# The FFN gate's modulation vector is computed during gate and up, by ScalarE and GpSimd

## The chip, the cores and the metric

The kernel runs on one core of one Trainium2 chip. The metric is the device time of one execution in microseconds. Engines are named as the profile names them: PE is TensorE (PEld its weight loads), DVE is VectorE, ACT is ScalarE, POOL is GpSimd, SP is SyncE, which issues most of the DMAs.

## The reference

One layer of a hybrid backbone over 640 tokens (512 latent, 128 context), model width 2048, FFN width 5632, all in fp32:

```
mod = silu(c) @ w_mod + b_mod            # w_mod is 2048 x 12288: six vectors of 2048
sh1, sc1, g1, sh2, sc2, g2 = split(mod, 6)
h = rmsnorm(x) * (1 + sc1) + sh1
p = h @ w_in                              # then RWKV-7 mixing and gMLP
x = x + g1 * (mix @ w_out)
h = rmsnorm(x) * (1 + sc2) + sh2
ff = (silu(h @ w_ffn_gate) * (h @ w_ffn_up)) @ w_ffn_down
y = rmsnorm(x + g2 * ff)
```

mod is made twice, from c for the latent tokens and from c_ctx for the context tokens (v = 0 and 1 in the code). The vector of this case is the last one, g2, number 5: it is used in the last part of the down projection alone.

## The kernel before

**Stages.** (1) Norm of x and the modulation vectors 0 and 1, to 125 us. (2) The input projection, 125 to about 1060 us: 43 column blocks of w_in, four pieces each (`pieces`), multiplied by `win`; between the matmuls run the mixers of RWKV and gMLP, which a small planner in the kernel (`Mixer`, with costs per job and due times counted in matmul steps) interleaves. The modulation vectors 2, 4, 3 and 5 are made here too. (3) The recurrence, (4) the output projection, (5) gate and up, from about 1490 to 2590 us, (6) the down projection, (7) the final norm.

**fp32 by halves.** Wherever a weight is multiplied, it is cut into a high part (`hi`, a ScalarE cast to fp32r, L1465 in gate, up and down) and a low part (`lo`, VectorE: raw minus hi, L1466); the product is hi*x_hi + hi*x_lo + lo*x_hi (L1685, L1686, L1688). hi and lo have three buffers each.

**Modulation vectors in stage 2** (`mod_all`, L939; `load_mod`, L932). For each vector and each pair of 128-row blocks of w_mod, two DMAs of 1 MB bring 2 x 128 x 2048; 8 products with the two columns of silu(c) (`cT`) as weights add up in one PSUM bank (L948). Then the bias comes in, VectorE adds (L965), TensorE turns the rows into columns (L182) and VectorE copies them to `modc[g]`. `mod_all` is a generator; after each piece of w_in it is advanced by MODR = 1.36 steps on average, so that its 204 steps spread over the 160 pieces.

**Gate and up.** `seven` (L1659 on) computes the product of a pair of column blocks with seven instead of eight half products (Strassen's scheme in Winograd's form). One loop turn f handles one block of columns (f = 2 to 43; blocks 0 and 1 are done plainly): per turn 8 weight tiles of 128 x 512 are loaded (`load_w`, L1778; 13 buffers); GpSimd makes 8 combinations of them (`combined`, L1594: `t` and `raw` are outputs), 7 half products o = 0 to 6 follow with 2 parts each, 12 matmuls of 320 columns per part. The results in PSUM are joined in `Gate` (L1830 on), four products late (LAG): VectorE additions with a PSUM operand (L1847, L1851, L1855, L1857, L1861), two of SBUF alone (L1856, L1858), a silu on ScalarE (L1862), a VectorE product (L1863). After every second turn GpSimd makes four combinations of the results (`stores`, L1803 to L1810), and `part` cuts three of them into halves (L1823, L1824). The `yield` of `seven` stands after each half product, so the loop body there can slip in loads.

**Order.** Each engine and the queue of each issuer run in order. Outside the regions with a schedule by hand, the framework's planner sets that order: it places each instruction when its own model of times has the inputs ready, the earlier one in the program first, and adds the semaphores.

**What uses the vector.** `Last` and `End` (L1944, L1997) read `modc[5]` in the last chunk of the down projection.

Of the kernel before, what the change touches and what calls it, by code (L numbers as in the profile page):

```python
# [10 lines left out]
F32 = mybir.dt.float32  # L11
F32R = mybir.dt.float32r
BF16 = mybir.dt.bfloat16
AF = mybir.ActivationFunctionType
ALU = mybir.AluOpType
# [4 lines left out]
P = 128  # L20
D = 2048
KB = D // P
# [24 lines left out]
WAIT = 20  # L47
NW = 8
SUBST = 4.6
MODR = 1.36  # L50
NREC = 8
CHK = (3, 3, 4, 4, 4, 4)
POOLK = (3,)
# [36 lines left out]
def flow_step(ctx: ExitStack, tc, x_prompt, x_sample, state_rwkv, c, c_ctx, w_mod, b_mod,  # L90
# [3 lines left out]
    nc = tc.nc  # L94
    V, S, G, TE = nc.vector, nc.scalar, nc.gpsimd, nc.tensor
# [13 lines left out]
    def tpool(**a):  # L109
        if a.get("space") != DRAM:  # L110
            a["reuse_waits"] = "tile"
        return tc.tile_pool(**a)

    cp = ctx.enter_context(tpool(name="const", bufs=1))
    dp = ctx.enter_context(tpool(name="dram", bufs=1, space=DRAM))
    cbx = ExitStack()
    cb = cbx.enter_context(tpool(name="constb", bufs=1))
# [5 lines left out]
    for h in range(2):  # L123
# [8 lines left out]
                         op0=ALU.mult, op1=ALU.add)  # L132
# [6 lines left out]
    mhalf = cp.tile([P, 1], F32, name="mhalf")  # L139
# [7 lines left out]
    mix = cb.tile([P, 640], F32, name="mix")  # L147
    gs2 = mix[96:128, 0:T]
    modc = {g: cp.tile([P, KB, 2], F32, name=f"modc{g}") for g in (2, 3, 4, 5)}
    cT = cb.tile([P, 2 * KB + 32], F32, name="cT")  # L150

    d_o = dp.tile([KB, P, T], F32, name="d_o")
    d_x1 = dp.tile([KB, P, T], F32, name="d_x1")
# [25 lines left out]
    def mod_cols(pspool, ms, out, tag="pt"):  # L179
        pt = pspool.tile([P, 4, P], F32, tag=tag, name="ptm")  # L180
        for cb in range(4):
            TE.transpose(pt[:, cb, :], ms[:, cb * P:(cb + 1) * P], ident)  # L182
        src = pt.rearrange("p cb (j r) -> p j cb r", r=32)
        for v in range(2):
            V.tensor_copy(out.rearrange("p (j cb) v -> p j cb v", cb=4)[:, :, :, v],
                          src[:, :, :, v])
# [745 lines left out]
    def load_mod(g, kb):  # L932
        quad = cur["pool"].tile([P, 2, 4, 512], F32, tag=cur["raw"], name="wt", bufs=1)
        for u in range(2):
            nc.sync.dma_start(quad[:, u].rearrange("p j n -> p (j n)"),
                              w_mod[0, (kb + u) * P:(kb + u + 1) * P, g * D:(g + 1) * D])
        return quad

    def mod_all():  # L939
        for g in (2, 4, 3, 5):  # L940
            pm = cur["psum"].tile([P, 512], F32, tag="pmod", name=f"pm{g}")
            quad = load_mod(g, 0)
            for _ in range(4):
                yield
            for kb in range(0, KB, 2):
                for u in range(2):
                    for j in range(4):
                        TE.matmul(pm[32 * j:32 * j + 2, :], cT[:, 2 * (kb + u):2 * (kb + u) + 2], quad[:, u, j, :],  # L948
                                  start=(kb + u == 0), stop=(kb + u == KB - 1), tile_position=(0, 32 * j))
                for _ in range(2):  # L950
                    yield
                if kb + 2 < KB:
                    quad = load_mod(g, kb + 2)
                    for _ in range(4):
                        yield
            ms = cur["pool"].tile([P, 2, 4, 512], F32, tag=cur["raw"], name=f"ms{g}", bufs=1)[:, 0, 0, :]
            G.memset(ms, 0.0)
            for j in range(4):
                for v in range(2):
                    nc.sync.dma_start(ms[32 * j + v:32 * j + v + 1, :],  # L960
                                      b_mod[:, g * D + 512 * j:g * D + 512 * j + 512])
            yield
            yield
            for j in range(4):
                V.tensor_add(ms[32 * j:32 * j + 2, :], pm[32 * j:32 * j + 2, :], ms[32 * j:32 * j + 2, :])  # L965
            mod_cols(cur["tp"], ms, modc[g], tag=cur["tag"])
            yield
# [6 lines left out]
    g = 0  # L974
# [21 lines left out]
    def take(b, halves):  # L996

        mixA.finish(b - RAW)
        pr = bp.tile([P, T], F32, tag="praw", name="praw", bufs=RAW)
        for hf in range(2):  # L1000
            S.copy(pr[:, HALF * hf:HALF * hf + HALF], halves[hf])
        mixA.add(blocks[b][1](pr), blocks[b][2], wide[0] + 32 * RAW)
# [18 lines left out]
    for n, (b, q) in list(enumerate(pieces))[N0:]:  # L1021
# [4 lines left out]
        if q == 3:  # L1026
            take(b, halves)
        due += MODR
        while due >= 1.0:
# [442 lines left out]
    with ExitStack() as ph:  # L1472
# [6 lines left out]
                        in1=prm[:, C_N2:C_N2 + KB].unsqueeze(2).to_broadcast([P, KB, 2]), op=ALU.mult)  # L1479
# [51 lines left out]
        for hf in range(2):  # L1531
            s = slice(HALF * hf, HALF * hf + HALF)
            for m in range(KB):
                if hf or m >= AHEAD:
                    four_blocks(hf, m, 0)
                ps = four_blocks(hf, m, 1)
# [8 lines left out]
                if hf and m > 1:  # L1545
                    for kb in HALVES[m - 2:m - 1] if m < 14 else HALVES[2 * m - 16:2 * m - 14]:
                        first_half(kb)
                    if 4 <= m < 12:
                        j, i = divmod(m - 4, 2)
# [34 lines left out]
    pP = ctx.enter_context(tpool(name="pP", bufs=8, space=PSUM))  # L1584
# [121 lines left out]
    def load_down(s):  # L1706
        if s < len(steps):
            c, n = steps[s]
            for b, r, m in (("11", 0, 0), ("21", 1, 0), ("22", 1, 1), ("12", 0, 1)):
                raw = xap.tile([P, 4, P], F32, tag=next(wtags), name="rawd")  # L1710
                r0 = (starts[c] + r * NFF // 2) * P
                nc.sync.dma_start(raw[:, 0:CHK[c], :], w_ffn_down[
                    0, r0:r0 + CHK[c] * P, (2 * n + m) * P:(2 * n + m + 1) * P].rearrange("(k p) n -> p k n", p=P))
                WD[s, b] = raw
                yield
# [55 lines left out]
    def load_w(n):  # L1771
        if n < NFF:
            f = ORDER[n]
            for b, w, k0 in (("11", w_ffn_gate, 0), ("21", w_ffn_gate, 8), ("22", w_ffn_up, 8), ("12", w_ffn_up, 0)):
                for q in range(2):
                    raw = gu.tile([P, 4, P], F32, tag="raw", name="raw", bufs=RAWB)
                    r0 = (k0 + 4 * q) * P
                    nc.sync.dma_start(raw, w[0, r0:r0 + 512, f * P:f * P + P].rearrange("(k p) n -> p k n", p=P))  # L1778
                    WB[n, b, q] = raw
                    yield  # L1780
# [6 lines left out]
    gux = ExitStack()  # L1787
# [42 lines left out]
    class Gate:  # L1830
# [5 lines left out]
        def __call__(self, o, p):  # L1836
# [22 lines left out]
            elif o == 6:  # L1859
# [7 lines left out]
                if f % 2:  # L1867
                    stores(f // 2)

    dloads = itertools.chain(load_down(0), load_down(1))  # L1870
    first_blocks()
    for f in range(2, NFF):
        b = {n: [WB.pop((f, n, q)) for q in range(2)] for n in ("11", "12", "21", "22")}
        bs = b["11"], b["12"], b["21"], b["22"]
        for o in seven(*bs, lambda i, k: X[i, k], Gate(f)):
            if o == 2:
                loads = itertools.chain(loads, load_w(f + 2))
            if o > 2:
                next(loads, None)
                next(loads, None)  # L1880
            if f == NFF - 2 and o == 6:
                load(0, 1)
                load(0, 2)
            if f == NFF - 1:
                now(FIRST_OPS, o)
                if o > 3:
                    next(dloads)
    for _ in range(2):
        next(dloads)
    while hooks:  # L1890
        hooks.pop(0)()
    part(3)
# [238 lines left out]
    for t in (3, 4, 0, 1, 2):  # L2131
        for h in (1, 0):
            out = fin.tile([P, 4, 256], F32, tag=f"out{h}", name="out")
# [3 lines left out]
            else:  # L2137
                V.scalar_tensor_tensor(out=out, in0=src, scalar=rse[:, t:t + 1],
                                       in1=fg[:, 4 * h:4 * h + 4], op0=ALU.mult, op1=ALU.mult)
# [31 lines left out]
```

## Time and profile before

| | us |
|---|---|
| median of 3 runs | 3196.04 |
| lowest and highest | 3189.53, 3201.81 |
| profiled execution, own time | 3191.31 |
| its span, first to last instruction | 3189.5 |

| engine | busy us | share of the span |
|---|---|---|
| PE | 3075.3 | 96% |
| DVE | 2347.6 | 74% |
| ACT | 1474.9 | 46% |
| POOL | 1220.2 | 38% |

The mean granted TensorE clock is 0.991. A row of a group reads: line, engine, operation, output<-inputs, shapes, count | busy us, mean ns of one | idle time of the engine just before these instructions, and what ended it. A row of the timeline reads: start, duration, engine, line, operation, tiles, count [idle time before <- what ended it]. Where instructions of one engine follow each other closely, their spans can overlap a little; start to start is then what one costs. A row of a stretch reads: from:to, length, then for each engine busy us and instructions, then granted clock, DMA share and GB/s.

### The profile page before, as it was taken

What the parts mean: (1) busy time and instruction counts of PE and PEld (TensorE: products, weight loads), DVE (VectorE), ACT (ScalarE), POOL (GpSimd) and SP (SyncE); (2) the same over time, 40 slices, a digit from 0 to 9 for tenths busy, and PEclk for the clock granted to TensorE, in tenths of its full rate; (3) what the DMA queues carried; (4) which work ended last, traced back from release to release, by engine and by line L of the source; (5) the groups of instructions that cost most, each with busy time, mean ns of one, the idle gap of its engine ahead of it and who ended that gap; (6) DMA issues with size and microseconds to landing.
All of it is one profiled execution on the core that took longest, in us unless ns stands there. A gap on an engine that the chain in (4) does not pass through costs nothing.

```text
span 3189.5 us, 72242 instructions
## 1 busy us (share of the span) xinstructions
PE 3075.3 (96%) x28216; PEld 2861.3 (90%) x28216; DVE 2347.6 (74%) x4120; ACT 1474.9 (46%) x3216; POOL 1220.2 (38%) x1065
## 2 busy tenths in 40 slices
PE   6899999999999999999999999999999999999997
PEld 4688878788878888899999999999999999999997
DVE  4566777667775678767877878777777788877788
ACT  3344544454444444346544444444444445444365
POOL 2001121221122024411465666656655655555542
PEclk9999999999999999999999999999999999999999
DMA  9767786777777688475344434443344365553453
GB/s 370 245 192 202 217 231 172 212 199 212 221 202 193 214 275 268 153 210 162 97 125 128 122 107 127 119 121 119 109 130 126 108 194 156 163 160 119 143 165 123
DMA packets 740439, 550.89 MB, mean 173 GB/s; under 512 B 141056, under 2 KB 673504, under 8 KB 731264
## 3 DMA queue, kind: packets, MB, share of 16 engines
q1 hardware_dynamic: 727136, 532.47, 55.3%
q0 software_dynamic: 10624, 13.23, 1.8%
q8 instruction: 222, 3.64, 0.5%
q14 instruction: 121, 0.99, 0.1%
q10 hardware_dynamic: 2336, 0.57, 0.1%
HBM read 437.79 MB, written 110.95 MB: 172 GB/s over the span
## 4 chain that ended last, share of the span: by engine, by line
PE 73%; DVE 10%; issue 6%; DMA 6%; ACT 3%; POOL 2%; SPq 0%; DVEq 0%; POOLq 0%; ACTq 0%
PE P L1688 15%; PE P L1685 15%; PE P L1686 15%; PE big L196 5%; PE big L200 4%; PE big L197 4%; DMA raw<-in_w_in_dram 1%; PE pm L948 1%; DVE lo L1466 1%; PE big L1081 1%; PE big L1524 1%; PE big L1525 1%; PE big L1526 1%; PE big L1082 1%; PE big L1083 1%
## 5 line engine op out<-in xcount | busy, mean ns | idle before, releaser
L1685 PE MATMUL P<-xo,hi 128*128 128x320 f32 x2352 | 700.5, 310 | 0.2 <-ACT hi L1465 0.2
L1686 PE MATMUL P<-xo,hi 128*128 128x320 f32 x2352 | 700.4, 309 | 0.0
L1466 DVE TENSOR_TENSOR lo<-raw,hi 128x512 fp32r<-128x512 f32 x526 | 517.8, 989 | 161.6 <-ACT hi L1465 158.7
L1465 ACT CAST hi<-raw 128x512 fp32r<-128x512 f32 x526 | 326.7, 622 | 468.4 <-PE P L1686 397.6
L1688 PE MATMUL P<-xo,lo 128*128 128x320 f32 x2352 | 441.8, 310 | 4.1 <-DVE lo L1466 4.1
L196 PE MATMUL big<-h_hi,hi 128*128 128x320 f32 x1376 | 438.2, 325 | 7.8 <-ACT hi L174 4.4
L1685 PEld LDWEIGHTS P<-xo,hi 128*128 128x128 f32 x2352 | 442.3, 188 | 0.5 <-ACT hi L1465 0.5
L1686 PEld LDWEIGHTS P<-xo,hi 128*128 128x128 f32 x2352 | 442.7, 188 | 0.0
L197 PE MATMUL big<-h_lo,hi 128*128 128x320 f32 x1376 | 422.6, 314 | 0.8 <-DVE h_lo L360 0.8
L1594 POOL TENSOR_TENSOR raw<-raw 128x512 f32<-128x512 f32 x252 | 410.5, 1638 | 10.1 <-DVE lo L1466 1.8
L1688 PEld LDWEIGHTS P<-xo,lo 128*128 128x128 f32 x2352 | 370.0, 188 | 4.9 <-DVE lo L1466 4.9
L1685 PE MATMUL P<-xd,hi 128*128 128x320 f32 x1232 | 367.8, 310 | 6.1 <-ACT P L2079 2.8
L1686 PE MATMUL P<-xd,hi 128*128 128x320 f32 x1232 | 366.8, 309 | 0.0
L200 PE MATMUL big<-h_hi,lo 128*128 128x320 f32 x1376 | 319.8, 312 | 3.9 <-DVE lo L175 2.1
L196 PEld LDWEIGHTS big<-h_hi,hi 128*128 128x128 f32 x1376 | 261.8, 190 | 58.2 <-issue 26.1
L175 DVE TENSOR_TENSOR lo<-raw,hi 128x512 fp32r<-128x512 f32 x268 | 185.4, 695 | 157.6 <-ACT hi L174 153.9
L1594 POOL TENSOR_TENSOR t<-raw 128x512 f32<-128x512 f32 x84 | 123.7, 1472 | 427.5 <-DMA raw<-in_w_ffn_up_dram 415.9
L1465 ACT CAST hi<-rawd 128x512 fp32r<-128x512 f32 (+1 forms) x288 | 167.1, 586 | 225.3 <-PE P L1686 148.9
L174 ACT CAST hi<-raw 128x512 fp32r<-128x512 f32 x268 | 164.4, 617 | 225.9 <-PE big L197 84.9
L197 PEld LDWEIGHTS big<-h_lo,hi 128*128 128x128 f32 x1376 | 261.6, 190 | 5.8 <-DVE h_lo L360 1.9
L1466 DVE TENSOR_TENSOR lo<-rawd,hi 128x512 fp32r<-128x512 f32 (+1 forms) x288 | 231.9, 812 | 24.9 <-ACT hi L1465 24.2
L1688 PE MATMUL P<-xd,lo 128*128 128x320 f32 x1232 | 236.6, 310 | 4.2 <-DVE lo L1466 4.2
(408 smaller groups left out, 6129.7 us busy)
## 6 DMA issues: line engine op xcount, KB each, us to landing
wt<-in_w_mod_dram SPq DMA_DIRECT2D x96, 1024.0 KB
raw<-in_w_ffn_gate_dram SPq DMA_DIRECT2D x182, 256.0 KB
raw<-in_w_ffn_up_dram SPq DMA_DIRECT2D x182, 256.0 KB
rec<-d_S SPq DMA_DIRECT2D x80, 576.0 KB
raw<-in_w_in_dram SPq DMA_DIRECT2D x172, 256.0 KB
rawd<-in_w_ffn_down_dram SPq DMA_DIRECT2D x128, 256.0 KB
raw<-in_w_out_dram SPq DMA_DIRECT2D x96, 256.0 KB
xd<-d_os SPq DMA_DIRECT2D x66, 320.0 KB
```

Of the source, the lines that this page charges most:

```text
L174: S.copy(hi, raw)
L175: V.tensor_sub(lo, raw, hi.bitcast(F32))
L196: TE.matmul(halves[hf], hi[:, k, :], h_hi[:, kb, s], start=(kb == 0), stop=False)
L197: TE.matmul(halves[hf], hi[:, k, :], h_lo[:, kb, s], start=False, stop=False)
L200: TE.matmul(halves[hf], lo[:, j - 4 * q, :], h_hi[:, j, s], start=False, stop=(j == KB - 1))
L948: TE.matmul(pm[32 * j:32 * j + 2, :], cT[:, 2 * (kb + u):2 * (kb + u) + 2], quad[:, u, j, :], start=(kb + u == 0), stop=(kb + u == KB - 1) ...
L1465: S.copy(hi[:, 0:nk], raw[:, 0:nk])
L1466: V.tensor_sub(lo[:, 0:nk], raw[:, 0:nk], hi[:, 0:nk].bitcast(F32))
L1594: G.tensor_tensor(out=o[:, 0:nk], in0=p[:, 0:nk], in1=q[:, 0:nk], op=ALU.subtract)
L1685: TE.matmul(ps, hi[:, k, :], xk[:, 0, :], start=q == 0 and k == 0 and not filled, stop=False)
L1686: TE.matmul(ps, hi[:, k, :], xk[:, 1, :], start=False, stop=False)
L1688: TE.matmul(ps, lo[:, k, :], x(i, 4 * q + k)[:, 0, :], start=False, stop=q == nq - 1 and k == nk - 1 and last)
```

## The change

Vector 5 leaves `mod_all`; MODR falls from 1.36 to 1.02, which is 1.36 x 3/4. `cT` moves from a pool that closes before gate and up to one that stays. A new generator `gate_mod` makes the vector in gate and up, a quarter (512 channels) at a time. For each of the 16 blocks of 128 rows it loads a 128 x 512 tile of w_mod (256 KB, three buffers, two steps ahead); for each v ScalarE multiplies the tile by the column of silu(c) (one value per partition) and GpSimd adds it to an accumulator `am` (128 x 512, fp32, with the bias in its first row). v = 0 writes a tile of its own (`wc`, one buffer), v = 1 writes over the loaded tile. After 16 blocks, 8 products of 128 x 128 pieces of the accumulators with a column of -0.5 sum over the partitions, in a PSUM bank of the pool that the half products use, and VectorE multiplies by -2 into `modc[5]`. The generator has 36 steps per quarter, and the loop advances it at o = 0, 2, 4, 6; what is left after the last turn is run there.

```
-MODR = 1.36
+MODR = 1.02
...
-    cT = cb.tile([P, 2 * KB + 32], F32, name="cT")
+    cT = cp.tile([P, 2 * KB + 32], F32, name="cT")
...
-        for g in (2, 4, 3, 5):
+        for g in (2, 4, 3):
...
+    gm = gux.enter_context(tpool(name="gm", bufs=1))
+    def gate_mod():
+        ws = []
+        def fetch():
+            i = len(ws)
+            if i < 4 * KB:
+                j, kb = divmod(i, KB)
+                w = gm.tile([P, 512], F32, tag="wm", name="wm", bufs=3)
+                nc.sync.dma_start(w, w_mod[0, kb * P:kb * P + P, 5 * D + 512 * j:5 * D + 512 * j + 512])
+                ws.append(w)
+        fetch()
+        fetch()
+        for j in range(4):
+            ac = [gm.tile([P, 512], F32, tag=f"am{v}", name="am") for v in range(2)]
+            for a in ac:
+                G.memset(a, 0.0)
+                nc.sync.dma_start(a[0:1, :], b_mod[:, 5 * D + 512 * j:5 * D + 512 * j + 512])
+            for _ in range(3):
+                yield
+            for kb in range(KB):
+                fetch()
+                w = ws[KB * j + kb]
+                for v in range(2):
+                    wc = w if v else gm.tile([P, 512], F32, tag="wc", name="wc")
+                    S.activation(wc, w, AF.Copy, scale=cT[:, 2 * kb + v:2 * kb + v + 1])
+                    G.tensor_tensor(out=ac[v], in0=ac[v], in1=wc, op=ALU.add)
+                    yield
+            yield
+            ps = pP.tile([P, 512], F32, tag="P", name="pgm")
+            for k in range(4):
+                for v in range(2):
+                    TE.matmul(ps[:, 2 * k + v:2 * k + v + 1], ac[v][:, P * k:P * k + P], mhalf, start=True, stop=True)
+            V.tensor_scalar(modc[5][:, 4 * j:4 * j + 4, :].rearrange("p k v -> p (k v)"), ps[:, 0:8], -2.0, None,
+                            op0=ALU.mult)
+    gmod = gate_mod()
...
+            if o % 2 == 0:
+                next(gmod, None)
...
+    for _ in gmod:
+        pass
```

## The prediction

> **What bounds the kernel now.** First the busy time by stretch, for the two stages that the change touches: the input projection (125 to 1030 us), which loses work, and gate and up (1560 to 2480 us), which gets it.
>
> ```profile
> core 0: us, PE busy (x) PEld busy (x) DVE busy (x) ACT busy (x) POOL busy (x), PEclk, DMA share, GB/s
> 125.00:1030.00 905.00, 873.99 (x10139) 750.95 (x10139) 627.69 (x1257) 440.81 (x936) 155.39 (x255) 0.99 0.73 204
> 1560.00:2480.00 920.00, 920.00 (x6264) 920.00 (x6263) 707.21 (x879) 396.63 (x690) 567.60 (x374) 1.00 0.40 119
> ```
>
> TensorE sets the pace of both: 97% busy in the first, without a gap in the second, at granted clock 1.00. One column block f of gate and up is 7 products x 2 parts x 12 = 168 matmuls, so 6264 matmuls are 37.3 blocks and one block takes 920/37.3 = 24.67 us. VectorE (77%), ScalarE (43%) and GpSimd (62%) look as if they had room there. Whether GpSimd's room is real is the question of this case, so next come the groups of that stretch.
>
> ```profile
> L1466 DVE TENSOR_TENSOR lo<-raw,hi 128x512 fp32r<-128x512 f32 x448 | 450.6, 1010 | 140.1 <-ACT hi L1465 137.5 <-issue 0.4
> L1594 POOL TENSOR_TENSOR raw<-raw 128x512 f32<-128x512 f32 x226 | 368.6, 1641 | 7.2
> L1594 POOL TENSOR_TENSOR t<-raw 128x512 f32<-128x512 f32 x75 | 109.5, 1459 | 346.2 <-DMA raw<-in_w_ffn_up_dram 334.8 <-DVE lo L1466 7.6 <-DVE act L1824 2.1
> L1465 ACT CAST hi<-raw 128x512 fp32r<-128x512 f32 x446 | 277.2, 622 | 414.3 <-PE P L1686 358.8 <-issue 17.7 <-POOL raw L1594 15.5
> L1824 DVE TENSOR_TENSOR act<-act,sp 128x320 fp32r<-128x320 f32 x57 | 47.3, 829 | 0.0
> L1857 DVE TENSOR_TENSOR pq<-P,pq 128x320 f32<-128x320 f32 x37 | 18.2, 491 | 1.3
> L1803 POOL TENSOR_TENSOR s<-act 128x320 f32<-128x320 f32 x19 | 24.8, 1308 | 0.0
> ```
>
> VectorE's subtraction for the low part (L1466, two operands in SBUF) has a mean of 1010 ns. The timeline of VectorE shows what it takes undisturbed: it starts, and 0.60 us later the next instruction does.
>
> ```profile
> 1823.36 0.48 DVE L1824 TENSOR_TENSOR act<-act,sp 128x320 fp32r<-128x320 f32 x1
> 1823.76 0.48 DVE L1851 TENSOR_TENSOR act<-P,act 128x320 f32<-128x320 f32 x1
> 1824.16 0.68 DVE L1466 TENSOR_TENSOR lo<-raw,hi 128x512 fp32r<-128x512 f32 x1
> 1824.76 0.48 DVE L1824 TENSOR_TENSOR act<-act,sp 128x320 fp32r<-128x320 f32 x1
> ...
> 1829.57 0.83 DVE L1863 TENSOR_TENSOR act<-act,c 128x640 f32<-128x640 f32 x1 [0.21 <-ACT c L1862]
> 1830.31 0.69 DVE L1466 TENSOR_TENSOR lo<-raw,hi 128x512 fp32r<-128x512 f32 x1
> 1831.90 1.22 DVE L1466 TENSOR_TENSOR lo<-raw,hi 128x512 fp32r<-128x512 f32 x1 [0.91 <-ACT hi L1465]
> ```
>
> In the quiet part of these rows GpSimd rests, by the first of its own rows for 8.38 us up to 1831.26:
>
> ```profile
> 1831.26 1.30 POOL L1594 TENSOR_TENSOR t<-raw 128x512 f32<-128x512 f32 x1 [8.38 <-DMA raw<-in_w_ffn_up_dram]
> 1832.52 1.33 POOL L1803 TENSOR_TENSOR s<-act 128x320 f32<-128x320 f32 x1
> ```
>
> Where it works back to back, the same instruction comes every 8.61/5 = 1.72 us (1.71 without the tail of the last), and GpSimd's own subtraction every 6.87/4 = 1.72:
>
> ```profile
> 1937.51 8.61 DVE L1466 TENSOR_TENSOR lo<-raw,hi 128x512 fp32r<-128x512 f32 x5
> ```
>
> ```profile
> 1935.29 6.87 POOL L1594 TENSOR_TENSOR raw<-raw 128x512 f32<-128x512 f32 x4
> ```
>
> So the two take turns on something, 0.60 us the one and 1.71 - 0.60 = 1.11 us the other, and do not overlap. Instructions that read PSUM are not held up: L1857 keeps a mean of 491 ns against 0.48 undisturbed, while L1824, with both operands in SBUF, has 829 against 0.48.
>
> The Trainium skill, page "SBUF — State Buffer", section "Who interferes with whom", states this as a rule: a VectorE instruction with two SBUF inputs and a GpSimd instruction that reads SBUF need one shared port, held by one of them for the whole instruction. The rows agree (1.71 is the sum, not the larger of the two). It speaks against putting additions on GpSimd here: by it the change costs at least the +23 us worked out below, by a port that both could read through at once it would cost nothing there.
>
> **The change, part by part.**
>
> *Taken from the input projection.* For g = 5: eight pairs of 1 MB loads, 8 x 16 matmul instructions (L948), four transposes (L182), small bias loads, four VectorE additions on two partitions. TensorE's timeline shows one such group and the transposes of one vector:
>
> ```profile
> 749.11 0.30 PE L533 MATMUL pmm<-lsum,bones 128*128 128x320 f32 x1
> 749.34 1.90 PE L948 MATMUL pm<-wt,cT 128*2 128x512 f32 x16
> 751.17 0.42 PE L196 MATMUL big<-h_hi,hi 128*128 128x320 f32 x1
> 751.43 0.31 PE L197 MATMUL big<-h_lo,hi 128*128 128x320 f32 x1
> ```
>
> ```profile
> 793.09 0.60 PE L182 MATMUL ptm<-ident,ms 128*128 128x128 f32 x4
> ```
>
> From L533 to L197 is 2.32 us; the two matmuls that start in it besides the group need 0.146 each (24.67/168), so the group costs 2.03 us. Eight make 16.2 us, with the transposes 16.8. MODR 1.02 spreads three vectors over the same blocks, so nothing gets denser. TensorE is 97% busy in this stage, so I take all of it: **-16.8 us**. Bounds: 0 if other waits fill it, -24 if the idle time ahead of L948 goes too, (71.8 + 25.0)/4:
>
> ```profile
> L948 PE MATMUL pm<-wt,cT 128*2 128x512 f32 x512 | 71.8, 592 | 0.0
> L948 PEld LDWEIGHTS pm<-wt,cT 128*2 128x2 f32 x512 | 10.3, 83 | 25.0 <-issue 24.1 <-PE big L197 0.2
> ```
>
> *Added to gate and up.* The generator advances at o = 0, 2, 4, 6, four steps per block; 36 steps make a quarter, so 144 steps fill 36 blocks, f = 2 to 37. Most steps are one ScalarE multiply (128x512) and one GpSimd addition (128x512). In the 36 blocks:
>
> ScalarE, at L1465's 622 ns, gets 4 x 0.62 = 2.5 us per block; 43% busy becomes 53%, and it waits for TensorE before most casts anyway (358.8 us of its idle time). Cost 0 while that cover holds.
>
> GpSimd gets four additions with two SBUF operands, like L1594. I count the shared resource per block of 24.67 us. GpSimd has 8 wide subtractions ((226 + 75)/37.3) and 2 narrow ones (four per two blocks). VectorE has 14 L1466, 1.5 L1824, L1856, L1858 and L1863. A wide pair is 1.71. A narrow GpSimd instruction holds 0.73: L1803 ends at 1832.52 + 1.33 = 1833.85, and VectorE's 1831.90 instruction before it ended at 1833.12.
>
> Before: 8 x 1.71 + 2 x (0.73 + 0.60) + 4 further L1466 x 0.60 + 3.5 x 0.40 + 0.74 = 13.7 + 2.7 + 2.4 + 2.1 = 20.9 us of 24.67. After: the four L1466 that stood alone become pairs, 12 x 1.71 + 2.7 + 2.1 = 25.3 us. That is more than the 24.67 that TensorE needs: the port becomes the bound, by 0.6 us per block at the least. VectorE has five additions per block that read PSUM (L1847, L1851, L1855, L1857, L1861), 5 x 0.40 (L1851 above) = 2.0 us; they leave the port free, and only those that fall into a GpSimd turn are hidden. GpSimd's turns are then 10.3 + 4.4 = 14.7 us, some 57% of a block, so 43% of 2.0 = 0.9 us is exposed: 26.2 us. Ends: 25.3 (all hidden) and 27.3 (none). Per block +1.5 us, times 36: **+55 us**; ends +23 and +95. The low parts have three buffers, so VectorE can fall behind by about two parts (3.5 us) before TensorE stands, which is gone within three blocks. TensorE's gaps should then stand ahead of L1688, released by L1466.
>
> On the rate of one addition the Trainium skill's page "GPSIMD Engine Reference", section 4.1, says GpSimd is about twice as slow as VectorE for two inputs; an estimate from that is 1.20 us per turn, 25.7 us per block at the least and 14 us more in all. The row's 1.11 is used.
>
> SyncE gets 64 loads of 256 KB and 8 of 2 KB. With three buffers, a load waits for the last addition of the tile three before; behind it stand the weight loads (L1778), which mostly wait for VectorE themselves, and for those GpSimd waits (334.8 us at t, above). 16.8 MB over 36 blocks add 18 GB/s to 119. I cost this at 0; if GpSimd's turn comes later for it, that is part of the upper end.
>
> ```profile
> SPq L1778 <- DVE lo L1466: 355.5, 186, 10.8
> ```
>
> Four times, TensorE runs 8 products with one column, whose weights are the accumulators. Each is two matmul instructions (L948: 512 for 256 calls); at L182's 0.15 us, 64 make 9.6 us. While TensorE waits for VectorE anyway they cost nothing; in a stage that it bounds, up to 9.6 us. They also wait for the last addition, one step earlier in the program, and hold one of eight PSUM banks: 0 to one GpSimd turn of 1.7 us each, 0 to 7 us; taken as 0. The move of cT issues nothing. The 8 memsets on GpSimd are some 0.5 us each, over 900 us: 0.
>
> *Sum.* 3191.3 (the profiled execution's own time) - 16.8 + 55 = 3229.5 us. The median of the runs shown, 3196.0, lies 4.7 above that execution; on its scale the forecast is **3234 us**.
>
> **The rivals.**
>
> *The port has room after all* (not slower). The sequence 1.71 was seen for five turns at most; if GpSimd slips its additions into VectorE's idle time (140 us ahead of L1466 in 920), blocks stay at 24.67. For it: VectorE is 77% busy. Against: free port time is 24.67 - 20.9 = 3.8 us, and 4.4 are wanted. Time: -16.8 + about 7 for the small products, 3181.5, on the median's scale 3186. It decides if the real turn is below 3.8/4 = 0.95 us.
>
> *The loads matter more* (faster). 16.8 MB leave a stage whose DMA share is 73%, and ScalarE waits there for weights:
>
> ```profile
> ACT hi L174 <- DMA raw<-in_w_in_dram: 74.6, 31, 8.0
> ```
>
> With -24 and a free port: 3191.3 - 24 + 7, scaled 3179 us, less if some of the 31 us in which TensorE idles there go too. Against: TensorE's idle time there is 3% in all.
>
> *Queues block each other* (much slower). A ScalarE multiply whose tile or buffer is late stands ahead of the casts, and a GpSimd addition that waits for it ahead of the combinations that TensorE needs at o = 3 to 6. Then VectorE's PSUM additions hide nothing: 27.3 us per block, +95: 3191.3 - 16.8 + 95, scaled 3274 us, and 3284 where the small products (9.6) are not hidden either. For it: all four engines are tied in one loop; against: ScalarE is half idle.
>
> *Nothing is saved in the input projection*, because waits fill the 16.8 us, and the port binds: 3251 us.
>
> **How the numbers follow.** Forecast (25.3 to 26.8 us per block; 3202 to 3256) 0.44; port free 0.27; blocked queues 0.14; loads 0.08; nothing saved 0.07. What a measurement of this kernel can tell from no change is about 0.5%, 16 us: 3180 to 3212 is "same". The port-free case lies in it for the most part, at its lower edge; a fifth of the forecast's range does too. Faster: the loads case and a fifth of the port-free one, 0.14; same: the rest of the port-free one and the lower edge of the forecast, 0.25; slower 0.61. Range: 3174 (the loads case with 5 us of TensorE's idle time on top) to 3284 (blocked queues, nothing hidden); the forecast's own range is 3202 to 3256.
>
> **What would show it.** Right: in gate and up TensorE is no longer 100% busy, with idle time ahead of L1688 put down to L1466; VectorE above 90%; L1466's mean near 1.4 us; the 37 blocks take some 55 us more, while the input projection ends 15 to 17 us earlier. Wrong: TensorE still without gaps there, L1466 longer but always in time; or gaps of several us at the casts or the combinations, put down to ScalarE's multiply or the loads of w_mod, which would be the blocked queues; or an input projection as long as before.

## The result: 4% slower, and the profile after

The changed kernel takes 3327.36 us (median of 4 runs, 3318.54 to 3330.67). Against the kernel before, run on the same chip, that is a ratio of 1.0405, with a 95% interval of 1.0375 to 1.0435. It is slower, as forecast, but by 131 us (from the median of 3196.04 shown above) instead of 38, and it lies 43 us above the upper end of the range. The profiled execution took 3330.67 us.

The first three parts of the page of the kernel after: span, busy time by engine, and the slices.

```profile
span 3328.9 us, 72583 instructions
...
PE 3123.8 (94%) x28148; PEld 2903.5 (87%) x28148; DVE 2367.9 (71%) x4118; ACT 1552.9 (47%) x3344; POOL 1405.9 (42%) x1200
...
PE   6999899999999999998999799799799999999997
...
POOL 2002121211121133225766856866865655555542
PEclk9999999999999999998999899899899999999999
```

No engine is full. But in gate and up TensorE's row has three single sevens (slices 23, 26 and 29), and in the same three slices GpSimd's row has its only eights. Something comes in bursts. The busy time by stretch, for the same two stretches as in the prediction:

```profile
125.00:1030.00 905.00, 862.85 (x9971) 749.91 (x9971) 622.33 (x1238) 441.28 (x934) 154.23 (x254) 0.97 0.68 184
...
1560.00:2480.00 920.00, 848.27 (x5452) 832.93 (x5452) 644.15 (x778) 417.49 (x727) 646.76 (x445) 0.95 0.40 120
```

The input projection had 97% TensorE before and has 95% after losing work (862.85 against 873.99 us). In gate and up TensorE does 5452 matmuls in 920 us instead of 6264. Where in these 920 us they are missing, shorter stretches of the same view show (columns as before: PE, PEld, DVE, ACT, POOL, then granted clock, DMA share, GB/s):

```profile
1810.00:1900.00 90.00, 69.55 (x393) 65.45 (x393) 48.98 (x55) 43.67 (x75) 73.15 (x55) 0.87 0.41 124
1900.00:2070.00 170.00, 170.00 (x1161) 170.00 (x1161) 128.18 (x162) 72.77 (x126) 104.66 (x69) 1.00 0.39 118
2070.00:2150.00 80.00, 60.44 (x334) 56.60 (x334) 40.08 (x41) 38.65 (x67) 72.81 (x54) 0.85 0.35 107
2150.00:2330.00 180.00, 180.00 (x1233) 180.00 (x1232) 137.76 (x178) 77.78 (x137) 111.58 (x74) 1.00 0.42 127
2330.00:2410.00 80.00, 60.63 (x330) 56.40 (x329) 45.98 (x47) 38.75 (x66) 70.29 (x52) 0.83 0.38 115
```

Between the bursts nothing is lost: 1161 matmuls at 0.1468 us (24.67/168) are 170.4 us of 170. In the bursts 393 matmuls are 57.7 us of 90, 334 are 49.0 of 80, and 330 are 48.4 of 80: 32.3 + 31.0 + 31.6 = 95 us lost in 250 us. The granted clock falls to 0.87, 0.85 and 0.83 there; (1 - clock) times the length is 11.7 + 12.0 + 13.6 = 37 us, so nearly two fifths of the loss is a TensorE that works at a lower clock. The rest is waiting: its busy time falls short of the three lengths by 20.5 + 19.6 + 19.4 = 59 us.

What GpSimd does in a burst stands in the rows of the tile `am`, the accumulator (duration in ns least/median/most, first and last start; the last row is the span in 40 slices):

```profile
L1900 POOL TENSOR_TENSOR am<-am,wc x64: 1252/1288/6672, 1527.6 to 2394.2; 128x512 f32<-128x512 f32 x64
L1900 POOL TENSOR_TENSOR am<-am,wm x64: 1257/1630/1818, 1532.3 to 2395.9; 128x512 f32<-128x512 f32 x64
...
L1906 PE MATMUL pgm<-mhalf,am x64: 165/250/250, 1814.1 to 2583.2; 128*128 128x1 f32 x64
L1890 POOL MEMSET am<- x8: 522/526/537, 1502.5 to 2330.7; 128x512 f32 x8
...
busy tenths in 40 slices 0000000000000000003201400500500000000000
```

The additions aren't spread over 36 blocks. They stand in four places, two slices wide at most, and the last of them starts at 2395.9 us, 187 us before the last small product. The planner sets each engine's order by when inputs are ready. All that a quarter's additions need is its tiles and its two accumulators, and these come free with the small products of the quarter before. So a quarter's 16 tiles run in one go as soon as the small products of the last one are through, while the small products themselves keep their place in the program. The times fit this: the small products stand at 1814, 2071, 2326 and 2582 us, and the second and the third burst begin some 11 us behind the first and the second of them. That the order makes the bursts is shown by spread, below. The timeline of all engines inside the second burst, with most rows left out:

```profile
1844.93 0.64 PE L1685 MATMUL P<-xo,hi 128*128 128x320 f32 x1 [2.18 <-ACT hi L1465]
1845.36 0.47 PE L1686 MATMUL P<-xo,hi 128*128 128x320 f32 x1
1845.63 0.47 PE L1685 MATMUL P<-xo,hi 128*128 128x320 f32 x1
...
1847.72 1.75 POOL L1900 TENSOR_TENSOR am<-am,wc 128x512 f32<-128x512 f32 x1
...
1849.42 1.28 POOL L1900 TENSOR_TENSOR am<-am,wm 128x512 f32<-128x512 f32 x1
1849.50 0.72 ACT L1899 ACTIVATE wc<-wm,cT 128x512 f32<-128x512 f32 x1 [1.54 <-POOL am L1900]
1850.13 0.60 ACT L1465 CAST hi<-raw 128x512 fp32r<-128x512 f32 x1
...
1850.78 0.41 PE L1685 MATMUL P<-xo,hi 128*128 128x320 f32 x1 [0.63 <-ACT hi L1465]
```

ScalarE's multiply into `wc` (L1899) waits 1.54 us for the addition (L1900) that still reads the one buffer. Behind it in ScalarE's order stands the cast (L1465, 1850.13), and TensorE, at 1850.78, waits for that cast. The first rows show the clock's part: after a wait of 2.18 us the matmuls start 0.27 us apart instead of 0.146. The sums, from the waits of the kernel after between 1490 and 2560 us (total us, times, longest):

```profile
ACT wc L1899 <- POOL am L1900: 124.5, 54, 7.3
PEld P L1685 <- ACT hi L1465: 65.2, 29, 4.5
PE P L1685 <- ACT hi L1465: 57.1, 27, 4.2
...
PEld P L1688 <- DVE lo L1466: 18.9, 23, 2.8
```

The forecast had the gaps ahead of L1688, put down to VectorE. They are ahead of L1685, put down to ScalarE, which waits for GpSimd.

The whole difference of the spans, 139.4 us, splits by the first matmul of `seven` (L1685 on `xo`) and the first of the down projection (L1685 on `xd`). Rows of those two tiles, kernel before, then kernel after:

```profile
L1685 PE MATMUL P<-xo,hi x2352: 305/309/468, 1549.7 to 2591.9; 128*128 128x320 f32 x196
...
L1685 PE MATMUL P<-xd,hi x1232: 302/309/418, 2592.8 to 3171.9; 128*128 128x320 f32 x176
```

```profile
L1685 PE MATMUL P<-xo,hi x2352: 302/309/637, 1567.6 to 2727.7; 128*128 128x320 f32 x196
...
L1685 PE MATMUL P<-xd,hi x1232: 302/309/418, 2728.6 to 3311.3; 128*128 128x320 f32 x176
```

Up to `seven` the kernel lost 17.9 us (1567.6 - 1549.7) where it should have gained; from there to the down projection 117.9 (1161.0 against 1043.1); after it 3.6. Of the 17.9, some 5 are there at the end of the input projection (last L196: 1059.8 before, 1064.8 after), and the rest is the first burst, which falls on the two plain blocks. Below, "the gate stage" is the time from first `xo` to first `xd`.

### The profile page after: what moved, and what is told of

It is laid out like the page before. It is cut to its first block, busy times and chain, and to the rows that moved or that the text cites. A ratio compares the mean times of both kernels' runs of the same rounds, so it can differ in the third digit from the quotient of the medians.

```text
span 3328.9 us, 72583 instructions
## 1 busy us (share of the span) xinstructions
PE 3123.8 (94%) x28148; PEld 2903.5 (87%) x28148; DVE 2367.9 (71%) x4118; ACT 1552.9 (47%) x3344; POOL 1405.9 (42%) x1200
## 3 DMA queue, kind: packets, MB, share of 16 engines
q14 instruction: 124, 1.02, 0.1%
## 4 chain that ended last, share of the span: by engine, by line
PE 49%; POOL 7%; DVE 6%; issue 6%; DMA 4%; ACT 2%; SPq 0%; DVEq 0%; POOLq 0%; ACTq 0%
PE P L1688 13%; PE P L1685 13%; PE P L1686 13%; POOL am L1900 3%; DVE lo L1466 2%; POOL raw L1594 1%; PE big L196 1%; PE big L1524 1%; PE big L1526 1%; PE big L1525 1%; PE big L200 1%; PE big L197 1%; PE big L1081 1%; DMA raw<-in_w_ffn_up_dram 1%; POOL t L1594 1%
## 5 line engine op out<-in xcount | busy, mean ns | idle before, releaser
L1685 PE MATMUL P<-xo,hi 128*128 128x320 f32 x2352 | 720.2, 317 | 57.1 <-ACT hi L1465 57.1
L1686 PE MATMUL P<-xo,hi 128*128 128x320 f32 x2352 | 715.1, 315 | 0.0
L1466 DVE TENSOR_TENSOR lo<-raw,hi 128x512 fp32r<-128x512 f32 x526 | 520.7, 996 | 236.9 <-ACT hi L1465 232.8
L1465 ACT CAST hi<-raw 128x512 fp32r<-128x512 f32 x526 | 324.8, 619 | 403.4 <-PE P L1686 338.7
L1685 PEld LDWEIGHTS P<-xo,hi 128*128 128x128 f32 x2352 | 454.8, 193 | 66.1 <-ACT hi L1465 65.2
L1688 PE MATMUL P<-xo,lo 128*128 128x320 f32 x2352 | 453.7, 316 | 13.6 <-DVE lo L1466 13.5
L1686 PEld LDWEIGHTS P<-xo,hi 128*128 128x128 f32 x2352 | 455.2, 194 | 0.0
L196 PE MATMUL big<-h_hi,hi 128*128 128x320 f32 x1376 | 438.2, 325 | 4.6 <-ACT h_hi L359 2.9
L1594 POOL TENSOR_TENSOR raw<-raw 128x512 f32<-128x512 f32 x252 | 399.6, 1595 | 10.9 <-DVE lo L1466 2.9
L1688 PEld LDWEIGHTS P<-xo,lo 128*128 128x128 f32 x2352 | 378.9, 193 | 19.9 <-DVE lo L1466 19.8
L1685 PE MATMUL P<-xd,hi 128*128 128x320 f32 x1232 | 367.9, 310 | 6.4 <-ACT hi L1465 2.2
L196 PEld LDWEIGHTS big<-h_hi,hi 128*128 128x128 f32 x1376 | 263.0, 191 | 47.0 <-issue 27.2
L1465 ACT CAST hi<-rawd 128x512 fp32r<-128x512 f32 (+1 forms) x288 | 167.1, 586 | 225.4 <-PE P L1686 152.8
L174 ACT CAST hi<-raw 128x512 fp32r<-128x512 f32 x268 | 164.7, 618 | 223.5 <-PE big L197 99.7
L1594 POOL TENSOR_TENSOR t<-raw 128x512 f32<-128x512 f32 x84 | 127.0, 1512 | 334.0 <-DMA raw<-in_w_ffn_up_dram 327.1
L1466 DVE TENSOR_TENSOR lo<-rawd,hi 128x512 fp32r<-128x512 f32 (+1 forms) x288 | 225.4, 789 | 25.5 <-ACT hi L1465 24.8
L1688 PE MATMUL P<-xd,lo 128*128 128x320 f32 x1232 | 236.9, 310 | 5.5 <-DVE lo L1466 5.2
```

The lines of the kernel that those rows point to most:

```text
L174: S.copy(hi, raw)
L196: TE.matmul(halves[hf], hi[:, k, :], h_hi[:, kb, s], start=(kb == 0), stop=False)
L1465: S.copy(hi[:, 0:nk], raw[:, 0:nk])
L1466: V.tensor_sub(lo[:, 0:nk], raw[:, 0:nk], hi[:, 0:nk].bitcast(F32))
L1594: G.tensor_tensor(out=o[:, 0:nk], in0=p[:, 0:nk], in1=q[:, 0:nk], op=ALU.subtract)
L1685: TE.matmul(ps, hi[:, k, :], xk[:, 0, :], start=q == 0 and k == 0 and not filled, stop=False)
```

## The experiments

Open after the result: is it the **order** (bursts), ScalarE's **multiply** with its single buffer, GpSimd's **additions** as such, or the **port** that VectorE and GpSimd share? And why did the input projection give nothing back? All kernels are variants of the changed one; the first edits differ from it, the later ones from the variant named.

### The steps held where the source puts them (`spread`)

```
-                    S.activation(wc, w, AF.Copy, scale=cT[:, 2 * kb + v:2 * kb + v + 1])
+                    tc.keep_in_program_order(
+                        S.activation(wc, w, AF.Copy, scale=cT[:, 2 * kb + v:2 * kb + v + 1]))
```

> The changed kernel, with each multiply of gate_mod pinned in ScalarE's program order behind the instruction traced before it, so that the steps are spread over the blocks f = 2 to 37 as the source has them, instead of four bursts of about 80 us. Theory of the bursts (ScalarE's multiply waits for GpSimd's addition, the casts wait behind it, because 16 steps' worth of additions come at once): without bursts the 36 blocks stay at or near 24.67 us, total 3195 to 3215. Theory of the shared port as predicted: every one of the 36 blocks takes 25.3 to 27.3 us, +23 to +95 us over a gate and up without the vector, total 3220 to 3295, idle time of TensorE ahead of L1688.

Measured: 3277.36 us, ratio 1.0241 (1.0224 to 1.0258). Its stretch, its waits (1560 to 2480 us) and the slices of `am`:

```profile
1560.00:2480.00 920.00, 867.94 (x5774) 845.96 (x5774) 745.56 (x806) 421.59 (x752) 700.72 (x465) 1.00 0.42 126
```

```profile
ACT hi L1465 <- POOL raw L1594: 127.8, 59, 3.1
PEld P L1688 <- DVE lo L1466: 64.7, 63, 1.5
PE P L1688 <- DVE lo L1466: 48.0, 61, 1.3
...
PEld P L1685 <- ACT hi L1465: 7.1, 12, 1.1
```

```profile
busy tenths in 40 slices 0000000000000000000122222222222000000000
```

This is the kernel that the prediction worked out, and it behaves as it said in kind: the additions are even, the gaps move to L1688 <- L1466, and none is longer than 1.5 us, so the clock stays at 1.00. Without the 48 small products in the stretch, 5726 matmuls in 920 us make a block 920 x 168 / 5726 = 27.0 us (forecast 26.2, ends 25.3 and 27.3). The rival that its expectation named, 24.67 us per block as soon as the bursts are gone (3195 to 3215 us), did not happen. The order alone costs 3327.36 - 3277.36 = 50 us, and the even version is still 2.4% slower than before.

### One part left out: additions (`noadd`), multiplies (`nomul`), all of it (`proj`)

```
noadd: -                    G.tensor_tensor(out=ac[v], in0=ac[v], in1=wc, op=ALU.add)
nomul: -                    wc = w if v else gm.tile(...)
       -                    S.activation(wc, w, ...)
       +                    wc = w
proj:  -    gmod = gate_mod()
       +    V.memset(modc[5], 0.5)
       +    gmod = iter(())
```

> The changed kernel without GpSimd's 128 additions (left out, so the vector is the bias alone); loads, multiplies and products stay. Theory of the bursts: nothing holds the one wc buffer any more, the casts are not held up, gate and up is back to 24.7 us a block, total 3195 to 3210. Rival, the 64 loads in SyncE's queue or the 128 multiplies themselves cost the time: total above 3260.

> The changed kernel without ScalarE's 128 multiplies (left out; GpSimd adds the loaded tiles as they are). If the loss comes from the casts queued behind a waiting multiply on ScalarE, it falls to under a third: total below 3245. If it comes from GpSimd itself, whose additions come in a burst ahead of the combinations or block VectorE at the port, it stays above two thirds: total above 3285. In between, both.

> The changed kernel without gate_mod: vector 5 is left out altogether (a constant instead), MODR 1.02, three vectors in the input projection. As predicted for the removed work: 16.8 us less than before, about 3180. As the changed kernel's trace has it (its input projection ended 5 us later than before, with TensorE idle or at half clock where it had the work): 3190 to 3205, no gain.

Measured: noadd 3211.67 and nomul 3321.95 us (one run each); proj 3189.23 us, ratio 0.9976 (0.9963 to 0.9988). The stretch of noadd, and waits of nomul between 1490 and 2560 us:

```profile
1560.00:2480.00 920.00, 913.58 (x6212) 909.89 (x6212) 670.93 (x866) 454.88 (x791) 558.20 (x374) 1.00 0.44 132
```

```profile
ACT hi L1465 <- POOL raw L1594: 107.2, 17, 29.9
...
PE P L1685 <- ACT hi L1465: 70.9, 6, 25.5
```

And in nomul's second burst, a run of additions on GpSimd, then the cast on ScalarE that waits for a combination behind it:

```profile
1845.70 23.95 POOL L1899 TENSOR_TENSOR am<-am,wm 128x512 f32<-128x512 f32 x18
```

```profile
1877.41 0.62 ACT L1465 CAST hi<-raw 128x512 fp32r<-128x512 f32 x1 [29.95 <-POOL raw L1594]
```

Without the additions 116 of the 131 us are gone; without the multiplies 5. So ScalarE's wait at `wc`, the largest new wait of the kernel after, is no cause: it passes on that GpSimd is late. Without it the same time shows up elsewhere, as single stalls of TensorE of up to 25.5 us, behind a cast that waits up to 29.9 us for a combination (L1594) which stands in GpSimd's order behind a run of 18 additions. Those take 23.95/18 = 1.33 us each, little more than the 1.25 us that the shortest one of the kernel after took, so there it is GpSimd's queue, and hardly the port, that holds TensorE up. In noadd the gate stage is still 1058.8 us against 1042.2 in proj; about 7 of these 16.6 us are the small products (next part), and the rest was not taken apart. For proj, 3180 was expected if the removed work came back whole, and 3190 to 3205 if none did; 3189.23 lies next to the latter.

### The port or GpSimd's time (`writes`), and half of the additions (`half`)

Both are spread otherwise. In writes, each addition is replaced by three memsets of the accumulator; by their rows below these are 3 x 0.527 = 1.6 us of GpSimd in place of the 1.65 to 1.71 us of an addition, but they only write. In half, the generator is advanced at o = 0 and 4 alone, and makes two quarters of the vector.

```
writes: -                    G.tensor_tensor(out=ac[v], in0=ac[v], in1=wc, op=ALU.add)
        +                    for _ in range(3):
        +                        tc.keep_in_program_order(G.memset(ac[v], 0.0))
half:   -            if o % 2 == 0:
        +            if o % 4 == 0:
        ...
        -        for j in range(4):
        +        for j in range(2):
```

> As the run spread, but each addition on GpSimd is replaced by three memsets of an accumulator (0.53 us each, 1.6 us together, as long as a contended addition); they only write, and the sums are left out. Theory of the shared port (GpSimd's reads and VectorE's second operand exclude each other): memsets do not block, blocks at 24.7 to 25.0 us, total 3195 to 3212. Rival, GpSimd's time and its queue (combinations late because other work stands ahead of them): blocks as in spread, 26.9 us and more, total above 3250.

> As the run spread, at half the rate: steps at o = 0 and 4 alone, two additions per block, and only the first two quarters of the vector (the others are left out, a constant). By the port 20.9 + 2 x 1.11 = 23.1 us plus at most 0.9 exposed, below 24.67: no block longer than 25.0 us but the two with the small products, total 3190 to 3202. Rival, each addition costs its share (spread lost 80 us for 128): total above 3225.

Measured (one run each): writes 3195.83, half 3196.85 us. The stretch of writes and GpSimd's groups in it:

```profile
1560.00:2480.00 920.00, 920.00 (x6290) 920.00 (x6290) 707.33 (x877) 471.27 (x815) 735.36 (x759) 1.00 0.44 136
```

```profile
L1594 POOL TENSOR_TENSOR raw<-raw 128x512 f32<-128x512 f32 x225 | 352.1, 1572 | 6.0
L1901 POOL MEMSET am<- 128x512 f32 x381 | 198.9, 527 | 14.5
```

GpSimd is busier than in spread (735 against 701 us), with the same loads and multiplies beside it, and TensorE hasn't a gap. It is not GpSimd's time or its queue that costs 27.0 us per block when the steps are even; it is that the additions read SBUF. (A memset also waits for no multiply, as an addition does; but in spread these waits are small, 14.1 us of ScalarE's for additions and 13.8 us of GpSimd's for multiplies.) The Trainium skill, page "SBUF — State Buffer", section "Who interferes with whom", states this as a rule: a VectorE instruction with two SBUF inputs contends with a GpSimd instruction that reads SBUF, not with one that only writes it. The memsets agree: they take 527 ns in the middle of VectorE's work, and 526 in the row of the kernel after, and L1466 on `raw` has a mean of 963 ns beside them (1010 before).

The gate stage of half takes 1046.1 us, 3.9 more than proj, with two sets of small products; that of writes 1049.1, 6.9 more, with four. That the small products are this difference, TensorE's timeline in writes shows:

```profile
1776.01 1.84 PE L1907 MATMUL pgm<-mhalf,am 128*128 128x1 f32 x16
1777.71 0.39 PE L1685 MATMUL P<-xo,hi 128*128 128x320 f32 x1
```

From the first of a set to the next matmul it is 1.70 us. So a set costs 1.7 to 1.9 us, and two additions per block cost nothing beside them. By the prediction's sum two additions fit (20.9 + 2 x 1.11 = 23.1 of 24.67 us) and four don't (25.3).

### The additions on VectorE (`dveadd`, `dvestt`, `dve35`) and shared (`mix35`)

dveadd is spread with V in place of G. In dvestt one VectorE instruction multiplies and adds, and ScalarE does nothing. dve35 and mix35 advance the generator 3.5 times per block instead of 4; mix35 gives v = 0 to GpSimd and v = 1 to VectorE.

```
dveadd: -                    G.tensor_tensor(out=ac[v], in0=ac[v], in1=wc, op=ALU.add)
        +                    V.tensor_tensor(out=ac[v], in0=ac[v], in1=wc, op=ALU.add)
dvestt: +                    tc.keep_in_program_order(V.scalar_tensor_tensor(out=ac[v], in0=w,
        +                        scalar=cT[:, 2 * kb + v:2 * kb + v + 1], in1=ac[v], op0=ALU.mult, op1=ALU.add))
mix35:  +                    (V if v else G).tensor_tensor(out=ac[v], in0=ac[v], in1=wc, op=ALU.add)
        ...
dve35, mix35:
        -            if o % 2 == 0:
        +            if (f + o) % 2 == 0:
```

> As the run spread, with the 128 additions on VectorE instead of GpSimd. By the port: VectorE holds it for 0.60 us per addition instead of 1.11, 20.9 + 4 x 0.60 = 23.3 us per block, below the 24.67 of TensorE, so blocks at 24.7 to 25.1 us, total 3195 to 3215. Rival, VectorE's own time is the bound (77% busy before, four more instructions with their waits): blocks at 25.5 us or more, total above 3222.

> Multiply and addition in one VectorE instruction (tile times the column value plus the accumulator), 128 of them, each pinned in VectorE's program order; no ScalarE multiply and no GpSimd addition, loads and products as in the changed kernel. By the port 23.3 us per block as with the additions alone: total 3193 to 3212, the least that this place for the vector can cost. If VectorE is the bound: above 3222.

> As dveadd (all additions on VectorE), with 3.5 steps per block instead of 4. By the port 20.9 + 3.1 x 0.60 = 22.8 us: 3193 to 3206. If each addition costs its share whatever the rate, as in dveadd: 3208 to 3218.

> As the run spread, with the additions for the latent column on GpSimd and those for the context column on VectorE, and steps at every second half product (3.5 per block instead of 4, over all 42 blocks). By the port about 20.9 + 1.6 x (1.11 + 0.60) = 23.6 us per block: near the 24.67 but below it, blocks 24.6 to 25.2 us, total 3193 to 3208. If the bound is VectorE's time with its waits, as the 94% busy of dveadd suggests, it gains little on dveadd: 3208 to 3220.

| | us | ratio (interval) | gate stage us |
|---|---|---|---|
| proj, nothing computed | 3189.23 | 0.9976 (0.9963 to 0.9988) | 1042.2 |
| dveadd | 3213.38 | 1.0056 (1.0040 to 1.0071) | 1056.8 |
| dve35 | 3210.25 | 1.0053 (1.0037 to 1.0069) | 1060.8 |
| dvestt | 3217.59 | 1.0070 (1.0049 to 1.0091) | 1062.9 |
| mix35 | 3228.24 | 1.0105 (1.0086 to 1.0123) | 1081.9 |
| spread | 3277.36 | 1.0241 (1.0224 to 1.0258) | 1127.2 |

The stretch of dveadd:

```profile
1560.00:2480.00 920.00, 916.06 (x6236) 912.03 (x6235) 859.65 (x998) 463.19 (x808) 576.80 (x374) 1.00 0.45 135
```

The engine that looks fuller is the better place. VectorE goes from 77% to 93% busy and the gate stage gets 14.6 us longer than in proj, 6.9 of it small products. On GpSimd, 62% busy before, the same additions make it 85.0 us longer. Taking one turn at the port of an addition on VectorE as the 0.60 us of an undisturbed L1466, four make 20.9 + 4 x 0.60 = 23.3 us per block. The sum isn't all, though. With fewer steps per block (dve35) the stage should be shorter than in dveadd and is 4.0 us longer; without ScalarE's part (dvestt) it is 6.1 us longer. And for mix35 the sum gives 20.9 + 1.75 x (1.11 + 0.60) = 23.9, under 24.67, but the stage is 39.7 us longer than in proj, and the time lies above both ranges that were expected. Turns that fit on average may still come late near the limit; in mix35 ScalarE's multiplies and GpSimd's additions also wait more for each other (29.8 and 41.5 us, against 14.1 and 13.8 in spread). No run tells these two apart.

### The input projection (`modr`, `none`)

modr is proj with the old spacing; none is proj with vectors 2, 4 and 3 as constants too, so that nothing is left to space.

```
modr: -MODR = 1.02
      +MODR = 1.36
none: -        for g in (2, 4, 3):
      +        for g in ():
```

> As proj (vector 5 left out, a constant instead), with MODR back at 1.36: the three vectors are made in the first three quarters of the input projection, none in the last. If the 16.8 us came short (7.5) because of the spacing of the remaining work, the time differs from proj's 3189 by more than 6 us; if TensorE's waits for the mixers take the rest whatever the spacing, 3183 to 3195.

> As proj, with vectors 2, 3 and 4 left out of the input projection as well (constants instead): 67 us of TensorE's work less than before there. If TensorE's work sets that stage, as the prediction took it: 50 us below proj, about 3139. If the mixers' chains on VectorE and ScalarE set it and TensorE's freed time turns into waits: less than half of that, above 3164.

Measured: modr 3176.03 us, 0.9941 (0.9925 to 0.9958); none 3121.06 us, 0.9767 (0.9750 to 0.9784). The input projection of proj, then of modr:

```profile
125.00:1030.00 905.00, 866.06 (x10172) 754.00 (x10171) 625.83 (x1239) 444.68 (x942) 154.28 (x254) 0.99 0.69 186
```

```profile
125.00:1030.00 905.00, 873.84 (x10369) 763.12 (x10369) 631.29 (x1252) 448.78 (x952) 156.47 (x256) 0.99 0.69 186
```

Same work, 197 matmuls more in the same time: TensorE idles 39 us at 1.02 and 31 at 1.36, as before. A vector is worth (3176.03 - 3121.06)/3 = 18 us by none, and the fourth one as much: modr is the kernel before without vector 5, and lies 18 us below it. Of these 18 us, 3189.23 - 3176.03 = 13 are lost again by the wider spacing. With 1.36 the last of the three vectors' products (L948) starts at 777 us and what comes before that stands as it did; with 1.02 it starts at 991, and the small matmuls of the mixers wait at other places. The longest of TensorE's waits in proj, between 125 and 1050 us, is one that modr has only in parts of 0.9 us:

```profile
PE pG L679 <- DVE mx L850: 6.4, 1, 6.4
```

Why that order waits more was not isolated.

### Old spacing with the vector computed (`after136`, `spread136`, `dve136`)

Each is the kernel of that name, with MODR = 1.36 (dve136: dveadd).

> The changed kernel with MODR back at 1.36 and nothing else. If the spacing alone took the input projection's gain, it comes back whole whatever gate and up does: 11 to 13 us below the changed kernel (proj lost 13 us against modr), 3314 to 3317. If the bursts in gate and up differ by chance between compilations, the time departs from that by more than 10 us.

> As spread with MODR 1.36. Additive: 3277 - 13 = 3264. With the same 27 us per block while the additions last.

> As dveadd (spread, additions on VectorE) with MODR 1.36. The parts should add up: modr's 3176 plus what dveadd's gate and up takes more than proj's (1056.8 against 1042.2 us, 14.6): 3191, some 3 to 5 us below before, a tie within 0.5%. If the parts do not add up: above 3200.

Measured: after136 3312.64 us, 1.0367 (1.0352 to 1.0383); spread136 3255.76 (one run); dve136 3198.91, 1.0013 (0.9997 to 1.0029). Beside their twins at 1.02 that is 14.7, 21.6 and 14.5 us less: the spacing's price, three times more. By adding up the parts, 3264 was expected of spread136 and 3191 of dve136; both miss that by 8 us, in opposite directions, so the parts add up only to about that. The end of the projection (last L196) is 1040.9 to 1046.5 us in these three and modr, against 1059.8 before and 1050.7 to 1066.7 in the kernels with 1.02. dve136, the best of those that compute the whole vector, ties with the kernel before; none beats it. More buffers for `wc` were not tried.

## Why the prediction was wrong, and where it held

**The step that failed** is the one that places the work: "The generator advances at o = 0, 2, 4, 6, four steps per block; 36 steps make a quarter, so 144 steps fill 36 blocks". That is the order in the source. The planner's is 32 additions at a time. The row of `am` and spread show it: spaced as the prediction had them the additions cost 50 us less, and 3277.36 us lies inside the range. A sum over 36 blocks uses port time that additions in a burst never see. With the prediction's own figures a burst of about two blocks has 2 x 3.8 us free, and its 32 additions want 32 x 1.11 = 35.5: 28 us are lost, four times 112. Measured are 31 to 32 per burst. But GpSimd's queue alone gives the same. Its groups in the second burst, 1820 to 1890 us:

```profile
L1900 POOL TENSOR_TENSOR am<-am,wm 128x512 f32<-128x512 f32 x16 | 24.3, 1517 | 0.0
L1900 POOL TENSOR_TENSOR am<-am,wc 128x512 f32<-128x512 f32 x16 | 22.9, 1434 | 0.0
```

The 32 additions took 47.2 us, and in two blocks it had 2 x 9.4 us to spare before (38% of 24.67), which leaves 28. At the 1.25 us of the shortest additions the 32 would still need 40 us, 21 more than there was, so by this sum the queue alone is the greater part; nomul, with TensorE held up behind additions that ran almost undisturbed, agrees. In the order of the changed kernel no run tells the two apart; in the even order writes did it. The lowered clock, 37 us in three bursts, was in no term at all. It lies within those losses, so that 28 comes near 31 does not confirm either sum.

**The port** is right in kind and within its ends: 27.0 us per block where 26.2 was taken (ends 25.3 and 27.3), so about 84 us in 36 such blocks instead of 55; by the gate stages of spread and writes it is 78. The mis-sized term is the exposed part of VectorE's additions that read PSUM: 27.0 - 25.3 = 1.7 of 2.0 us if it is that alone, where 0.9 was taken. Two of the signs named failed even in spread, though. VectorE's groups in its stretch:

```profile
L1466 DVE TENSOR_TENSOR lo<-raw,hi 128x512 fp32r<-128x512 f32 x411 | 445.0, 1103 | 137.2 <-ACT hi L1465 134.9 <-POOL s L1803 0.8
L1824 DVE TENSOR_TENSOR act<-act,sp 128x320 fp32r<-128x320 f32 x51 | 77.3, 1516 | 0.0
...
L1856 DVE TENSOR_TENSOR act<-act,pq 128x320 f32<-128x320 f32 x34 | 44.8, 1318 | 0.0
```

VectorE is 81% busy there, not above 90%, and L1466's mean is 1.10 us, not 1.4; it is the narrow ones that grow (L1824 from 829 to 1516 ns). Much of the rest is a loop of waits (cast for combination, 127.8 us; silu for VectorE, 142.0), not a full engine. How the 1.7 us divide between the two stays open.

**The input projection**: the work's worth was right (16.8 forecast; 18 by none and modr), the step from "nothing gets denser" to "I take all of it" was not. Nothing got denser, and still 13 us went with the new order; the changed kernel even ended that stage 5 us later. A density is no order.

**ScalarE at 0** held: nomul takes away 5 us of 131, though a multiply took 0.72 us (the rows of L1899 above) where 0.62 was taken. **SyncE at 0** held in the even order (writes has all the loads, and 1049.1 us). **The small products at 0** did not: 6.9 us, within the ends of 0 and 9.6. They would hide only while TensorE waits anyway.

**The rivals.** "Queues block each other" came nearest. It had the sign, gaps at the casts, and GpSimd's additions ahead of the combinations that TensorE needs, which nomul shows. It had them wait for a late multiply, and that nomul rules out; and its price was taken for even steps as well, 27.3 us per block. "The port has room" fell with spread and writes. "Nothing is saved in the input projection" happened for more than half in proj (8 us of 18 left) and in full in the changed kernel. "The loads matter more" did not happen: ScalarE's wait for weights there (L174, 125 to 1030 us) did fall, from 40.7 to 16.8 us, and the stage still ended 5 us later. The chances do not add up as told: by the prediction's own parts "same" would get 0.30 and "slower" 0.56.

**The difference by measured terms**, for the even kernel: its span is 89.9 us longer than before. Up to `seven` that is 0.6 us (1550.3 against 1549.7), so nothing of the 16.8 came back; in the gate stage 84.1 (1127.2 against 1043.1), of which some 78 are the additions and some 7 the small products; after it 5.2, not taken apart. With the order, 50 more.

## What to carry to other kernels

Before an added loop is priced per block, ask who decides its order: where a planner places work by readiness, work that needs only loads and a free buffer runs in bursts, and its place in the source means little unless it is pinned. An engine's busy share does not tell whether there is room on it: for GpSimd beside VectorE count the turns at what they share, by the row of one undisturbed instruction and of one in a pair, and here that put the additions on the engine that was 77% busy, not on the one that was 62% busy. And price the prize first: with the vector not computed at all and the old spacing the kernel gains 0.6%, and the cheapest place found for it gave all of that back.

## What the runs showed of the hardware

A wait of a couple of us costs more than itself: in the three stretches of bursts shown, each of TensorE's 15 waits over 2 us (2.08 to 4.24) was followed, at once or within 1.8 us, by matmuls that started 0.27 us apart, and the granted clock was 0.83 to 0.87 over 80 to 90 us. Of the five waits of 1.4 to 1.8 us there, three were not followed by such matmuls within 4 us, and the many waits of up to 1.5 us in spread left the clock at 1.00. GpSimd memsets of 128x512 ran at 527 ns amid VectorE's work without delaying TensorE at all, while additions of the same size, 1.65 to 1.71 us each at even spacing, made the gate stage 78 us longer (1127.2 against 1049.1).
